# Sparse attention inside a hybrid layer: the products with the low parts of the keys contracted over 128 rows instead of 64

## The chip, the cores and the metric

One Trainium2 chip, one core of it. The metric is device time in microseconds (us) of one launch. The kernel before took 3008.09 us, the median of 3 runs (3004.27 to 3015.14). PE is TensorE (PEld its weight loads), DVE VectorE, ACT ScalarE, POOL GpSimd, SP SyncE; SPq is SP's DMA queue.

## What is computed

Two layers. Each layer norms 1104 token rows (16 meta tokens, 1024 prompt tokens, 64 sample tokens), projects them, and runs three branches: a gated linear recurrence, a convolution module, and an attention that keeps 256 keys a row by the scores of a small indexer. The parts of the reference that the change touches:

```
def index_scores(qi, wi, ki):
    s = jnp.einsum('bqhd,bsd->bqhs', qi.astype(F32), ki.astype(F32))
    return jnp.einsum('bqhs,bqh->bqs', jax.nn.relu(s), wi.astype(F32) * IDX_SCALE)
...
def sparse_attend(q, kg, vg, valid):
    nb, nq = q.shape[:2]
    qg = q.reshape(nb, nq, C_KV_HEADS, C_HEADS // C_KV_HEADS, C_HEAD_DIM).astype(F32)
    logits = jnp.einsum('bqhgd,bqnhd->bqhgn', qg, kg.astype(F32)) * (C_HEAD_DIM ** -0.5)
    logits = jnp.where(valid[:, :, None, None, :], logits, MASK_NEG)
    p = jax.nn.softmax(logits, axis=-1)
    o = jnp.einsum('bqhgn,bqnhd->bqhgd', p, vg.astype(F32))
    return o.reshape(nb, nq, C_WIDTH).astype(q.dtype)
```

A head has 64 channels (C_HEAD_DIM and IDX_DIM), there are 2 kv heads with 4 query heads each, and 4 index heads.

## The kernel before

**Split products.** All products keep float32 accuracy by halves: a value is split into a high part (rounded to fp32r) and a low part (what is left). A projection does three products for a tile: high with high, high with low, low with high. For queries and keys of 64 channels there is a denser form. The stationary operand is a *stack* of 128 rows, the high part of the query in one half of the rows and the low part in the other. The moving operand `KD` (`KIH` in the indexer) holds the high part of the keys in both halves, so one product over 128 rows gives (high + low query) x high key. A second product adds high query x low key: it takes the 64 rows of the stack with the high query, and the 64 rows of `KL` (`KIL`) with that head's low keys. It is this second product that contracts over 64 rows.

**Where it stands.** (1) `indexer`, lines 725 to 863: `qk` (768 to 771) writes the scores of one of 4 heads, for a tile of 128 query rows and up to 1024 keys, 512 at a time: line 770 is the product over 128 rows, 771 the one over 64. The row tiles go from i = 7 down to 2, with 128(i+1) keys each. `KIL` has the low keys in both halves already. Lines 861 and 862 do the same for the last 16 prompt rows. (2) `attention`, lines 945 to 1083: for i from 7 down to 0 and for the two kv heads k, `scores` (992 to 1016) does the 4 heads of the group, each in pieces of at most 512 keys (128 for i below 2); line 1004 is the product over 128 rows, 1005 the one over 64. `KL` is one tile: kv head 0 in rows 0 to 63, kv head 1 in 64 to 127. `queries(i)` (979 to 987) loads one tile of queries (`qr`, one buffer) and builds the stacks of both kv heads in one tile `Q`; it is called for i - 1 at the second kv head of i.

**Around it.** After a score piece DVE adds the mask and keeps the largest value (line 1011), from one of two PSUM banks (`sc`); ACT takes the exponential (204), DVE the reciprocal and the product with it (1014, 1015). `values` transposes the probabilities on PE (1023), ACT and DVE split them (1026, 1027) and PE multiplies them with the split values (1040, 1041). In the indexer ACT takes the relu (204, tile `rl`, two buffers) and DVE adds it up with its weight (803, 805); the taps of the convolution (1478, 1479) run on DVE in between.

**What sets the order.** PE's order is the program's, written by hand: tables of step counts (`FILL`, `SIDE`) say how many steps of the projections, three products each (line 391, later 326 to 328), stand behind each head's scores, each step of `values`, and so on. In `attention` DVE's order comes from a scheduler, as ACT's, POOL's and SP's do nearly everywhere; in the indexer DVE's is by hand too. Each queue runs strictly in its order.

Of the kernel before, what the change touches and what calls it, by code (L numbers as in the profile page):

```python
# [17 lines left out]
F32 = mybir.dt.float32  # L18
# [25 lines left out]
# steps of the projections that go at each place, and ns of the work of VectorE that does  # L44
# [18 lines left out]
def _layout():  # L63
# [11 lines left out]
    # channel-major, (half, chunk, kv head, 8) on the partitions  # L75
# [79 lines left out]
def trunk(tc, a, o, depth=DEPTH):  # L155
# [4 lines left out]
    def f(x):  # L160
        return x.bitcast(F32)
# [10 lines left out]
    # two banks, as one tile or as two  # L172
# [14 lines left out]
    def dmt():  # L187
        # where nothing else is under way: the slots of both tags
        return mmt() if next(turn) % 5 < 2 else tpt()
# [19 lines left out]
    # DRAM scratch  # L209
# [26 lines left out]
    # per-layer vectors, channel on the partition  # L236
# [5 lines left out]
    # lower bound of the gates of each layer  # L242
# [21 lines left out]
    def weights(l, blk, eng=None, pool=None):  # L264
        # 8 tiles of 128 x 128: the rows of one column chunk, or 4 row tiles of two column chunks
# [29 lines left out]
    class Early:  # L295
        # the products of the first two branches: they take the place of the rows, once no projection needs those
# [44 lines left out]
    def stream(l, pv, chunks, groups, slot, early, lead, more):  # L341
        # projections that wait in DRAM, one step (three products) at a time, after a first call for the weights alone;
        # the first `lead` chunks go by groups of tokens, as they are normalised, and so do the last two
# [19 lines left out]
        for i, g in parts:  # L363
# [16 lines left out]
            if i == 0:  # L380
                # the low parts of the rows come two of them behind
# [8 lines left out]
            for j, (w, x) in enumerate(ops):  # L390
                T.matmul(ps, w, x, start=(j == 0), stop=(j == 23))  # L391
                if j == 23:
                    # the gates of the first two branches as they are used, the others are activated later
                    fn = AF.Sigmoid if nm == "gate" and c < 16 else AF.Identity
                    act_(bufs[i][:, sl], ps, fn, bias=pv[:, bcol + c:bcol + c + 1])
                    if nm in ("cz",):
                        # stored as its silu
                        if g == 0:
                            sg = spt()
                        act_(sg[:, sl], ps, AF.Sigmoid, bias=pv[:, bcol + c:bcol + c + 1])  # L400
                        G.tensor_tensor(bufs[i][:, sl], bufs[i][:, sl], sg[:, sl], op=OP.mult)
# [8 lines left out]
    class Side:  # L410
        # work of VectorE that fits in anywhere, about `ns` of it at a time
# [42 lines left out]
    def inverse(parts, nn, tmp):  # L454
        # of the root of the mean square; roots and reciprocals are taken with the tokens on the partitions
# [19 lines left out]
    def norm_group(H, pv, g, r, tmp, pool="1357", lag=0):  # L475
        # a step for each row of tiles; the low parts `lag` of them behind
# [27 lines left out]
    def squares(g, out, lag=0):  # L504
        # the squares of a group of tokens, but for the last ones added up, `lag` of them behind
# [18 lines left out]
    def start(fill):  # L524
        # the first norm and the first projections, a group of tokens at a time
# [8 lines left out]
        for g in range(3):  # L534
            ahead = squares(g + 1, parts, 2) if g < 2 else iter(())
            for k, _ in enumerate(norm_group(H0, pvs[0][0], g, r, tmp0, "1346", 2)):
                next(ahead, None)
                # the rest of the products of the group before
# [15 lines left out]
    def constants():  # L554
        consts.update(cload(("rc", "rs", "cm80", "selw", "cols", "hsel", "bd", "p16"), "cb", S))
        # masks in fewer bytes: small numbers, or a far lower one
# [8 lines left out]
        # row of 8 cache slots held by partition p for sequence b: page_table[b, p // 16] * 16 + p % 16  # L565
# [7 lines left out]
    def layer(l, hst, late):  # L573
# [7 lines left out]
        # the last layer returns no outputs for the meta tokens  # L581
# [111 lines left out]
    def rope_q():  # L693
        # the rotated channels of all heads side by side, (half, chunk, kv head, 8) on the partitions
# [30 lines left out]
    def indexer(l, CTr, SC, SC8, fill, taps):  # L725
        with tc.tile_pool(name="ixc", bufs=1) as xc, tc.tile_pool(name="ixt", bufs=2) as xt:
# [3 lines left out]
            # high and low parts side by side  # L730
# [37 lines left out]
            def qk(dst, q, h, rows, c0, c1):  # L768
                j, e = divmod(h, 2)
                T.matmul(dst, q[:, j, e, 0:rows], KIH[:, c0:c1], start=True, stop=False)  # L770
                T.matmul(dst, q[64 * e:64 * e + 64, j, e, 0:rows], KIL[64 * e:64 * e + 64, c0:c1], start=False, stop=True)
# [37 lines left out]
            # last prompt rows and the sample rows  # L809
# [6 lines left out]
            # q stack of the tail rows: [hi; lo] for every head  # L816
# [43 lines left out]
            for (c0, c1), dst in zip(CH, (ps[0:64, 0:512], ps[0:64, 512:1024], px[0:64, 0:80])):  # L860
                T.matmul(dst, lq, KIH[:, c0:c1], start=True, stop=False)
                T.matmul(dst, lq[0:64], KIL[0:64, c0:c1], start=False, stop=True)
# [32 lines left out]
    def topk(SC, SC8, t1):  # L895
        # the 256th largest score of every row, bit by bit from the top of its float pattern
# [3 lines left out]
        def steps(j0, j1):  # L900
# [5 lines left out]
            for bit in range(31, -1, -1):  # L906
# [6 lines left out]
                # the bit stays, or goes back (the top one: to all ones); then the next one to try  # L913
# [7 lines left out]
    def topk_masks(SC, SC8, MB, MB8, F, t1):  # L921
        # 0 where a key is kept, MASK elsewhere; of equal scores the first ones are kept
# [22 lines left out]
    def attention(l, lo, MB, MB8, fill):  # L945
        with ExitStack() as st:
# [13 lines left out]
            KL = ac.tile([128, 1024], F32R, name="KL", tag="KL")  # L960
            for hf in range(2):
# [4 lines left out]
                for k in range(2):  # L966
# [3 lines left out]
                    V.tensor_tensor(KL[e, sl], ps[e], f(KD[k][e, sl]), op=OP.subtract)  # L970
            # high and low parts side by side: the rows of a head's own half of the products hold the high ones
# [7 lines left out]
            def queries(i):  # L979
                qr = at.tile([128, 4, 128], F32, name="qr", tag="qr", bufs=1)  # L980
                Y.dma_start(qr, fD["q"][:, :, 128 * i:128 * i + 128].rearrange("c p n -> p c n"))
                Q = at.tile([128, 2, 4, 128], F32R, name="Q", tag="Q")
                lo, hi = qr[0:64], qr[64:128]
                act_(Q[0:64, 0], lo, AF.Copy, scale=0.125)
                act_(Q[64:128, 1], hi, AF.Copy, scale=0.125)
                V.scalar_tensor_tensor(Q[64:128, 0], lo, 0.125, f(Q[0:64, 0]), op0=OP.mult, op1=OP.subtract)
# [772 lines left out]
```

## Time and profile before

| | |
|---|---|
| runs (us) | 3015.14, 3008.09, 3004.27; median 3008.09 |
| profiled execution, span | 3013.0 us, granted TensorE clock 0.980 on average |
| PE busy | 2881.1 us (96%), 17094 products |
| PEld busy | 2641.4 us (88%) |
| DVE busy | 2113.0 us (70%) |
| ACT, POOL busy | 1183.1 us (39%), 1250.3 us (41%) |
| line 1005 (attention, 64 rows) | 208 products, 88.8 us, mean 427 ns |

A busy PE is counted to the modelled end of each product, and products overlap, so its busy share says little of how closely they follow each other; the *starts* of two neighbours in the timeline do. The time of the profiled execution around its span is not listed apart; the highest of the three runs lies 2.1 us above the span, the median 4.9 us below it.

### The profile page before, as it was taken

The page shows a single profiled execution, that of the slowest core. Times are in us where ns is not written, and L with a number is a line of the kernel's source. Part 1 is how long each engine was busy: PE and PEld are TensorE (multiplying, and loading weights), DVE is VectorE, ACT ScalarE, POOL GpSimd, SP SyncE. Part 2 cuts the span into 40 slices and gives each one's busy share as a digit, 9 for nine tenths or more (in the row PEclk, how much of TensorE's full clock was granted, in tenths as well). Part 3 has the DMA queues.
Part 4 walks back from the last instruction along what each step waited for, and adds up shares of the span by engine and source line. Part 5 has one row for each costly group of instructions (what it writes and reads, how often), then busy time and mean ns, then how long its engine had stood idle before and what let it go on. Part 6 is the DMA issues. An engine that isn't in the chain of part 4 may idle for free. (4 is left out here: it accounts for less than half of the span.)

```text
span 3013.0 us, 44973 instructions
## 1 busy us (share of the span) xinstructions
PE 2881.1 (96%) x17094; PEld 2641.4 (88%) x17094; DVE 2113.0 (70%) x3824; ACT 1183.1 (39%) x2357; POOL 1250.3 (41%) x978
## 2 busy tenths in 40 slices
PE   8989999999999999989999999998999999999898
PEld 7988879999998888879999887898998988888798
DVE  5789768888978567444466895789898776664443
ACT  4323443333333456444441334422332244564432
POOL 3533334443434115746563332534452331157453
PEclk9999999999999999999999999999999999999999
DMA  4422333333244124655452312422331441246554
GB/s 150 150 82 83 102 107 128 113 122 115 82 154 149 59 81 138 209 170 185 156 165 79 110 66 100 157 74 99 122 132 64 155 142 58 76 146 209 170 159 152
DMA packets 192567, 374.13 MB, mean 124 GB/s; under 512 B 30656, under 2 KB 129696, under 8 KB 192288
## 3 DMA queue, kind: packets, MB, share of 16 engines
q1 hardware_dynamic: 166016, 272.21, 28.8%
q10 hardware_dynamic: 20448, 78.09, 6.4%
q0 software_dynamic: 5888, 20.97, 2.2%
q8 instruction: 134, 2.20, 0.3%
q14 instruction: 81, 0.66, 0.1%
HBM read 251.07 MB, written 122.40 MB: 124 GB/s over the span
## 5 line engine op out<-in xcount | busy, mean ns | idle before, releaser
L391 PE MATMUL mm<-xh,wh 128*128 128x384 f32 (+2 forms) x2656 | 891.8, 338 | 21.1 <-ACT sp L204 18.6
L391 PE MATMUL mm<-xl,wh 128*128 128x384 f32 (+2 forms) x2656 | 885.5, 336 | 0.0
L270 POOL TENSOR_TENSOR wl<-wr,wh 128x512 fp32r<-128x512 f32 x332 | 478.8, 1461 | 769.0 <-ACT wh L269 465.2
L391 PEld LDWEIGHTS mm<-xh,wh 128*128 128x128 f32 x2656 | 506.1, 191 | 38.9 <-ACT sp L204 22.9
L391 PE MATMUL mm<-xh,wl 128*128 128x384 f32 (+2 forms) x2656 | 533.8, 337 | 0.0
L391 PEld LDWEIGHTS mm<-xl,wh 128*128 128x128 f32 x2656 | 505.8, 190 | 7.6 <-issue 2.3
L391 PEld LDWEIGHTS mm<-xh,wl 128*128 128x128 f32 x2656 | 459.9, 192 | 9.5 <-issue 5.5
L910 DVE TENSOR_SCALAR_CACHE_REDUCE jk<-SC,F 80x1104 bf16<-80x1104 f32 (+6 forms) x448 | 448.7, 1002 | 8.4
L204 ACT ACTIVATE sp<-mm,vec 128x384 f32<-128x384 f32 (+1 forms) x356 | 198.6, 566 | 526.2 <-PE mm L391 509.4
L1478 DVE SCALAR_TENSOR_TENSOR cy<-up,vec,cy 128x1040 f32<-128x1040 f32 x240 | 329.2, 1372 | 0.4
L269 ACT CAST wh<-wr 128x512 fp32r<-128x512 f32 x352 | 203.9, 618 | 174.4 <-PE mm L391 90.4
L204 ACT ACTIVATE P<-P,nm 128x896 f32<-128x896 f32 (+7 forms) x128 | 99.6, 778 | 85.7 <-DVE nm L1011 84.5
L1027 DVE TENSOR_TENSOR pl<-tp,ph 128x512 fp32r<-128x512 f32 x144 | 98.2, 688 | 49.2 <-ACT ph L1026 48.7
L1479 DVE SCALAR_TENSOR_TENSOR cy<-us,vec,cy 128x64 f32<-128x64 f32 x240 | 123.3, 514 | 0.0
L1011 DVE CUSTOM_DVE_ANT_0 P<-sc,MB 128x512 f32<-128x512 f32 (+1 forms) x96 | 64.1, 668 | 80.5 <-PE sc L1005 80.3
L1026 ACT CAST ph<-tp 128x512 fp32r<-128x512 f32 x144 | 83.6, 584 | 89.0 <-PE tp L1023 85.6
L1329 PE MATMUL lg<-hQ,hK 128*128 128x64 f32 x512 | 68.5, 292 | 24.1 <-DVE hQ L1358 24.1
L1023 PE MATMUL tp<-ident,P 128*128 128x128 f32 x576 | 91.1, 280 | 0.5 <-DVE P L1015 0.5
L1329 PEld LDWEIGHTS lg<-hQ,hK 128*128 128x128 f32 x512 | 68.0, 210 | 26.3 <-issue 19.8
L1015 DVE TENSOR_SCALAR P<-P,nm 128x896 f32<-128x896 f32 (+7 forms) x128 | 85.8, 670 | 4.4
L1005 PE MATMUL sc<-KL,Q 64*128 64x512 f32 (+2 forms) x208 | 88.8, 427 | 0.0
L287 PE MATMUL tp<-xh,wh 128*128 128x384 f32 (+2 forms) x240 | 79.9, 335 | 0.4 <-DVE z L1664 0.4
(455 smaller groups left out, 5964.0 us busy)
## 6 DMA issues: line engine op xcount, KB each, us to landing
wr<-in_wp SPq DMA_DIRECT2D x180, 512.0 KB, 3.8
eg<-gateD SPq DMA_DIRECT2D x80, 184.0 KB, 3.0
gateD<-sp ACTq DMA_DIRECT2D x24, 552.0 KB, 2.7
gateD<-sp ACTq DMA_DIRECT2D x24, 544.0 KB, 2.7
cr<-in_wc SPq DMA_DIRECT2D x16, 290.0 KB, 3.2
gt<-gateD SPq DMA_DIRECT2D x24, 192.0 KB, 3.2
za<-zaD SPq DMA_DIRECT2D x24, 192.0 KB, 3.8
ggD<-sp ACTq DMA_DIRECT2D x8, 552.0 KB
```

What stands on the lines that cost most here:

```text
L204: S.activation(out, in_, fn, **kw)
L269: S.copy(wh[:, k:k + 4], wr[:, k:k + 4])
L270: (eng or G).tensor_tensor(wl[:, k:k + 4], wr[:, k:k + 4], f(wh[:, k:k + 4]), op=OP.subtract)
L391: T.matmul(ps, w, x, start=(j == 0), stop=(j == 23))
L910: V.tensor_scalar(jk[0:rows, 0:n], s, F.bitcast(F32)[0:rows, j:j + 1], None, op0=OP.is_ge, op1=OP.add, accum_out=cnt[0:rows, j:j + 1])
L1005: T.matmul(ps, Q[64 * k:64 * k + 64, k, c, :], KL[64 * k:64 * k + 64, c0:c1], start=False, stop=True)
L1015: V.tensor_scalar(p[:, 0:n], p[:, 0:n], nm[:, 3:4], None, op0=OP.mult)
L1023: T.transpose(ps[:, 128 * c:128 * c + 128], P[c][:, 128 * kt:128 * kt + 128], ident)
L1027: V.tensor_tensor(pl, ps, f(ph), op=OP.subtract)
L1329: T.matmul(ps[:, 64 * c:64 * c + 64], K[:, 128 * c:128 * c + 128], up(Q[:, 128 * c:128 * c + 128], m), start=True, stop=True)
L1478: V.scalar_tensor_tensor(yp, up[:, j:j + 1040], w, yp, op0=OP.mult, op1=OP.add)
L1479: V.scalar_tensor_tensor(ys, us[:, :, j:j + 8], w, ys, op0=OP.mult, op1=OP.add)
```

## The change

The second product of each pair runs over all 128 rows: the whole stack (high and low query) against the low keys in both halves. What it adds to the result is low query x low key. For the attention the low keys must stand in both halves for each kv head, so `KL` becomes two tiles `KL0`, `KL1` and each is written twice. The stack is built for one kv head at a time: `queries(i)` issues the load and gives back `halves`, which is called for k = 1 at the first kv head of i, and for k = 0 of i - 1, right after the load, at the second. `Q` keeps two buffers, each half as large. In the tail a scratch tile takes the place of `KL0` in place of `KL`. Comments went too, which moves line numbers from 965 on by 1, from 990 on by 4 and from 1064 on by 8.

```diff
             def qk(dst, q, h, rows, c0, c1):
                 j, e = divmod(h, 2)
                 T.matmul(dst, q[:, j, e, 0:rows], KIH[:, c0:c1], start=True, stop=False)
-                T.matmul(dst, q[64 * e:64 * e + 64, j, e, 0:rows], KIL[64 * e:64 * e + 64, c0:c1], start=False, stop=True)
+                T.matmul(dst, q[:, j, e, 0:rows], KIL[:, c0:c1], start=False, stop=True)
...
-                T.matmul(dst, lq[0:64], KIL[0:64, c0:c1], start=False, stop=True)
+                T.matmul(dst, lq, KIL[:, c0:c1], start=False, stop=True)
...
-            KL = ac.tile([128, 1024], F32R, name="KL", tag="KL")
+            KL = [ac.tile([128, 1024], F32R, name=f"KL{k}", tag=f"KL{k}") for k in range(2)]
...
                     V.tensor_copy(KD[k][64:128, sl], ps[e])
-                    V.tensor_tensor(KL[e, sl], ps[e], f(KD[k][e, sl]), op=OP.subtract)
+                    for d in (slice(0, 64), slice(64, 128)):
+                        V.tensor_tensor(KL[k][d, sl], ps[e], f(KD[k][d, sl]), op=OP.subtract)
...
-                Q = at.tile([128, 2, 4, 128], F32R, name="Q", tag="Q")
-                lo, hi = qr[0:64], qr[64:128]
-                act_(Q[0:64, 0], lo, AF.Copy, scale=0.125)
-                act_(Q[64:128, 1], hi, AF.Copy, scale=0.125)
-                V.scalar_tensor_tensor(Q[64:128, 0], lo, 0.125, f(Q[0:64, 0]), op0=OP.mult, op1=OP.subtract)
-                V.scalar_tensor_tensor(Q[0:64, 1], hi, 0.125, f(Q[64:128, 1]), op0=OP.mult, op1=OP.subtract)
-                return Q
+
+                def halves(k):
+
+                    Q = at.tile([128, 4, 128], F32R, name="Q", tag="Q")
+                    own, other = (slice(64 * e, 64 * e + 64) for e in (k, 1 - k))
+                    act_(Q[own], qr[own], AF.Copy, scale=0.125)
+                    V.scalar_tensor_tensor(Q[other], qr[own], 0.125, f(Q[own]), op0=OP.mult, op1=OP.subtract)
+                    return Q
+
+                return halves
...
-                    T.matmul(ps, Q[:, k, c, :], KD[k][:, c0:c1], start=True, stop=False)
-                    T.matmul(ps, Q[64 * k:64 * k + 64, k, c, :], KL[64 * k:64 * k + 64, c0:c1], start=False, stop=True)
+                    T.matmul(ps, Q[:, c, :], KD[k][:, c0:c1], start=True, stop=False)
+                    T.matmul(ps, Q[:, c, :], KL[k][:, c0:c1], start=False, stop=True)
...
-            Q = queries(7)
+            split = queries(7)
+            Q = split(0)
             fill("aq")
             for i in range(7, -1, -1):
                 oc = at.tile([128, 4, 128], F32, name="oc", tag="oc", bufs=1)
                 for k in range(2):
-                    if k:
-                        Qn = queries(i - 1) if i else None
+                    if k == 0:
+                        Qn = split(1)
+                    elif i:
+                        split = queries(i - 1)
+                        Qn = split(0)
...
-                Q = Qn
+                    Q = Qn
...
-            p = ac.tile([128, 1024], F32, name="p8", tag=("KL", "VS1")[gi % 2])
+            p = ac.tile([128, 1024], F32, name="p8", tag=("KL0", "VS1")[gi % 2])
```

PE's and POOL's instructions are as many as before, and PE's stand in the same order. The scheduler sets DVE, ACT and SP anew in the attention.

DVE, at the start of the attention of the first layer, from the first part of `KD` to the first mask of a score (`ISA`, line 1011, 1015 in the change). Before:

```order
L969 CAST KD_8532<-tp 64x512
L970 TENSOR_TENSOR KL<-tp,KD_8532 64x512
L969 CAST KD_8532<-tp 64x512
L970 TENSOR_TENSOR KL<-tp,KD_8532 64x512
L969 CAST KD_8533<-tp 64x512
L986 SCALAR_TENSOR_TENSOR Q<-qr,Q 64x512
L970 TENSOR_TENSOR KL<-tp,KD_8533 64x512
L969 CAST KD_8533<-tp 64x512
L987 SCALAR_TENSOR_TENSOR Q<-qr,Q 64x512
L970 TENSOR_TENSOR KL<-tp,KD_8533 64x512
L986 SCALAR_TENSOR_TENSOR Q<-qr,Q 64x512
L1011 ISA P,nm<-sc,MB 128x512
```

And in the change:

```order
L969 CAST KD_8532<-tp 64x512
L971 TENSOR_TENSOR KL_8534<-tp,KD_8532 64x512 x2
L969 CAST KD_8532<-tp 64x512
L971 TENSOR_TENSOR KL_8534<-tp,KD_8532 64x512
L969 CAST KD_8533<-tp 64x512
L971 TENSOR_TENSOR KL_8535<-tp,KD_8533 64x512 x2
L971 TENSOR_TENSOR KL_8534<-tp,KD_8532 64x512
L989 SCALAR_TENSOR_TENSOR Q<-qr,Q 64x512 x2
L969 CAST KD_8533<-tp 64x512
L971 TENSOR_TENSOR KL_8535<-tp,KD_8533 64x512 x2
L1015 ISA P,nm<-sc,MB 128x512
```

Four more subtractions into `KL` stand ahead of the first mask, and one piece of the stack less.

ACT, a little later in the same place, up to the second exponential (`P,nm<-P,nm`; `sp` are results of projections, `wh` high parts of weights). Before:

```order
L204 ACTIVATE Q<-qr 64x512
L269 CAST wh<-wr 128x512 x2
L204 ACTIVATE Q<-qr 64x512
L204 ACTIVATE sp<-mm,vec 128x336 x2
L204 ACT_TABLE_LOAD
L204 ACTIVATE P,nm<-P,nm 128x1024
L404 DMA czD<-sp 128x1104
L204 ACTIVATE P,nm<-P,nm 128x1024
```

And in the change:

```order
L204 ACTIVATE sp<-mm,vec 128x384 x2
L269 CAST wh<-wr 128x512 x2
L204 ACTIVATE sp<-mm,vec 128x336
L204 ACT_TABLE_LOAD
L204 ACTIVATE P,nm<-P,nm 128x1024
L204 ACT_TABLE_LOAD
L204 ACTIVATE sp<-mm,vec 128x336
L204 ACT_TABLE_LOAD
L204 ACTIVATE P,nm<-P,nm 128x1024
```

The stacks of the next row tile are gone from here; the first exponential comes between two `sp`, and two more loads of ACT's function table with it.

SP's queue, from the first output gate (`czt`) on. Before:

```order
L981 DMA qr<-qD 128x4x128
L1054 DMA czt<-czD 128x4x128
L267 DMA wr<-in_wp 128x1024
L981 DMA qr<-qD 128x4x128
L267 DMA wr<-in_wp 128x1024 x2
L1049 DMA ocD<-oc 128x4x128
L1054 DMA czt<-czD 128x4x128
L267 DMA wr<-in_wp 128x1024
L981 DMA qr<-qD 128x4x128
```

And in the change:

```order
L1058 DMA czt<-czD 128x4x128
L267 DMA wr<-in_wp 128x1024
L982 DMA qr<-qD 128x4x128
L267 DMA wr<-in_wp 128x1024 x2
L1053 DMA ocD<-oc 128x4x128
L1058 DMA czt<-czD 128x4x128
L982 DMA qr<-qD 128x4x128
L267 DMA wr<-in_wp 128x1024
```

The first `qr` of the rows before (the queries of tile 5) now stands behind that `czt` and a weight load, the second (tile 4) behind the store of an output (`ocD`) and the next `czt`; the third (tile 3) has left the piece.

## Rows read from the trace of the kernel before

**Rows 1.** The page's first part: span, and busy time of each engine.

```profile
span 3013.0 us, 44973 instructions
PE 2881.1 (96%) x17094; PEld 2641.4 (88%) x17094; DVE 2113.0 (70%) x3824; ACT 1183.1 (39%) x2357; POOL 1250.3 (41%) x978
```

**Rows 2.** Busy time by window: the first layer's indexer and attention.

```profile
core 0: us, PE busy (x) PEld busy (x) DVE busy (x) ACT busy (x) POOL busy (x), PEclk, DMA share, GB/s
230.00:336.00 106.00, 106.00 (x534) 88.41 (x534) 97.71 (x122) 40.71 (x72) 34.65 (x21) 1.00 0.24 81
956.00:1249.00 293.00, 290.46 (x1533) 242.24 (x1533) 180.31 (x437) 157.84 (x318) 94.81 (x78) 0.99 0.31 98
```

**Rows 3.** Waits, 956 to 1249 us: total us, times, longest us.

```profile
DVE P L1011 <- PE sc L1005: 52.6, 62, 3.2
...
PE sc L1004 <- DVE nm L1011: 0.5, 1, 0.5
```

**Rows 4.** One line's view: L1004 in 956 to 1249 us, L770 in the whole.

```profile
L1004 PE MATMUL sc<-KD,Q x104: 218/387/505, 956.0 to 1248.4; 128*128 128x512 f32 x48, 128*128 128x128 f32 x32, 128*128 128x384 f32 x16, 128*128 128x256 f32 x8
...
L770 PE MATMUL lg<-KIH,qs x80: 326/396/505, 230.0 to 1806.9; 128*128 128x512 f32 x48, 128*128 128x384 f32 x16, 128*128 128x256 f32 x8, 128*128 128x128 f32 x8
```

**Rows 5.** Timeline of PE, attention, i = 7: start, duration, line, tiles, rows*columns, shape.

```profile
986.06 0.39 PE L1004 MATMUL sc<-KD,Q 128*128 128x512 f32 x1
986.38 0.49 PE L1005 MATMUL sc<-KL,Q 64*128 64x512 f32 x1
986.80 0.49 PE L1004 MATMUL sc<-KD,Q 128*128 128x512 f32 x1
987.22 0.50 PE L1005 MATMUL sc<-KL,Q 64*128 64x512 f32 x1
987.65 0.66 PE L1023 MATMUL tp<-ident,P 128*128 128x128 f32 x4
988.06 0.48 PE L1040 MATMUL ac<-ph,VS 128*128 128x512 f32 x1
988.38 0.39 PE L1041 MATMUL ac<-pl,VS 128*128 128x512 f32 x1
988.61 0.34 PE L391 MATMUL mm<-xh,wh 128*128 128x384 f32 x1
```

**Rows 6.** Timeline of PEld, the same stretch.

```profile
986.38 0.18 PEld L1005 LDWEIGHTS sc<-KL,Q 64*128 64x128 f32 x1 [0.30 <-issue]
986.79 0.19 PEld L1004 LDWEIGHTS sc<-KD,Q 128*128 128x128 f32 x1 [0.24 <-issue]
...
988.15 0.19 PEld L1041 LDWEIGHTS ac<-pl,VS 128*128 128x128 f32 x1
```

**Rows 7.** Timeline of PE, the next such transposes, with no pair ahead of them.

```profile
989.67 0.60 PE L1023 MATMUL tp<-ident,P 128*128 128x128 f32 x4
...
990.56 0.34 PE L391 MATMUL mm<-xh,wh 128*128 128x384 f32 x1
990.74 0.34 PE L391 MATMUL mm<-xl,wh 128*128 128x384 f32 x1
```

**Rows 8.** Timeline of PE, i = 2: one pair of 384 columns, two projections.

```profile
1170.08 0.34 PE L1004 MATMUL sc<-KD,Q 128*128 128x384 f32 x1
...
1170.99 0.33 PE L327 MATMUL mm<-xl,wh 128*128 128x368 f32 x1
1171.15 0.33 PE L328 MATMUL mm<-xl,wl 128*128 128x368 f32 x1
```

**Rows 9.** Timeline of PE, i = 1: two pairs of 128 columns, one projection.

```profile
1197.22 0.22 PE L1004 MATMUL sc<-KD,Q 128*128 128x128 f32 x1
...
1198.41 0.33 PE L327 MATMUL mm<-xl,wh 128*128 128x368 f32 x1
```

**Rows 10.** Timeline of DVE, i = 6: the masks of one head's two pieces.

```profile
1001.76 0.69 DVE L1011 CUSTOM_DVE_ANT_0 P<-sc,MB 128x512 f32<-128x512 f32 x1 [0.73 <-PE sc L1005]
...
1002.60 0.62 DVE L1011 CUSTOM_DVE_ANT_0 P<-sc,MB,nm 128x384 f32<-128x384 f32 x1
```

**Rows 11.** Waits, 230 to 336 us.

```profile
DVE qs L764 <- ACT qs L763: 7.7, 4, 4.8
```

**Rows 12.** One line's view: L970, the low keys, on DVE.

```profile
L970 DVE TENSOR_TENSOR KL<-tp,KD x8: 682/689/695, 946.4 to 2448.0; 64x512 fp32r<-64x512 f32 x8
```

**Rows 13.** Timeline of ACT, first head of the attention.

```profile
959.81 1.28 ACT L204 ACT_TABLE_LOAD   x1
```

**Rows 14.** DMA issues: count, KB each, median us to landing.

```profile
qr<-qD SPq DMA_DIRECT2D x16, 256.0 KB, 3.0
```

**Rows 15.** Waits of SP's queue, 956 to 1249 us.

```profile
SPq L1049 <- POOL oc L1055: 32.7, 7, 21.1
```

## The prediction

> **What bounds the kernel now.** Read the page's first part before anything else: PE is counted busy for 96% of the span and DVE for 70% [rows 1]. That share is over all stages, so the next view is the busy time by window in the two stages that the change touches. There PE is busy for 106.00 of 106 us in the indexer and 290.46 of 293 in the attention of a layer, at a granted clock of 1.00 and 0.99 (the 2.4 GHz level); DVE is at 97.71 and 180.31 [rows 2]. Then the waits: in the attention DVE waits 52.6 us for line 1005, while PE waits for DVE's masks 0.5 us [rows 3]. So PE sets the pace in both stages, closely followed by DVE in the indexer and not in the attention.
>
> Next, how often the product with the low keys runs. Line 1004 and its partner 1005 come 104 times a layer, 48 times with 512 columns, 16 with 384, 8 with 256, 32 with 128; lines 770 and 771 come 80 times in both layers, 48, 16, 8 and 8 [rows 4].
>
> Last, what one pair costs, from the starts in PE's timeline. Two pairs of 512 columns at 986.06 and 986.80 hold PE until 987.65: starts 0.32, 0.42, 0.42 and 0.43 us apart. Yet lines 1040 and 1041, also 512 columns and also two products with the same stationary operand, show 0.23 from the second to its follower (988.38 to 988.61) [rows 5]. The weight loads tell why. Line 1041's load starts at 988.15, while line 1040, started at 988.06, is under way; those of 1005 and of the 1004 behind it start with their own product, after idle times of 0.30 and 0.24 us that the profile ascribes to nothing but issue [rows 6]. A load of the other row count waits until the product ahead is through, on the way into 64 rows and on the way back. That is the time the change can take.
>
> **What it removes.** I take the excess over the same rows without a switch. With four products at 0.23 the stretch from 986.06 to 987.65 (1.59 us) would take 0.92; the transposes and the value products behind it take 0.96 (987.65 to 988.61), and 0.89 where no pair stands ahead (989.67 to 990.56) [rows 5, 7]. So two pairs cost 0.67 + 0.07 = 0.74 too much, 0.37 a pair. For 384 columns: from the pair at 1170.08 through two projection products to 1171.15 is 1.07 us; at 0.17 for each of the four (a projection product of 384 columns follows its like by 0.18 [rows 7], one of 368 by 0.16 [rows 8]) it would be 0.68, an excess of 0.39 [rows 8]. For 128 columns: two pairs and one projection product take 1197.22 to 1198.41, 1.19 us; a product of 128 columns without a switch I put at 0.11, from four transposes in (0.89 - 0.46) / 4 [rows 7], so 4 x 0.11 + 0.16 = 0.60, an excess of 0.59, 0.29 a pair [rows 9]. For 256 columns I take 0.38, between its neighbours.
>
> Attention, a layer: 72 pairs of 256 columns or more x 0.38 + 32 x 0.29 = 27.4 + 9.3 = 36.7 us; two layers 73. Indexer, both layers: 80 x 0.39 (each head is followed by projections, so the price of rows 8) = 31 us. The six pairs of lines 861 and 862 I price likewise, 2 us. Gross 106 us.
>
> On the loads' overlap the Trainium skill says the opposite: "TensorE: Matmul & The Clock Gate", Part 3, has it that a weight load overlaps a running product only when their row groups differ. By that rule the wide product, which shares all rows with its partner, would expose its load as the narrow one does, and the gross sum would be 0 instead of 106. The trace disagrees: 1041's early load is of the same 128 rows [rows 6], and I take the trace.
>
> **What it adds.** The new second product has as many columns; its price of 0.23 is in the sum already. Losses, each against that sum:
>
> - *Masks of neighbouring heads.* The first two heads of a group stand nearly back to back on PE. With 0.46 a pair of pieces PE comes back to the two PSUM banks sooner than DVE has emptied them: a piece takes DVE 0.84 [rows 10]. Two heads of two pieces need 2 x 0.92 + 0.5 of projection work on PE, against 1.4 us until the first bank and 2.3 until the second is free; a wait of 0.3 to 0.5 us for i = 7, 6, 5, both kv heads: 2.4 us a layer, 5 in all. Below: nothing, where fill steps cover it; above: 0.84 for each of 16 groups and two layers, 27.
> - *Indexer and DVE.* DVE is busy 97.71 of 106 us there and idle 8.3, of which 7.7 is waiting for ACT's share of the query stacks, itself behind PE [rows 2, 11]. Without 15.6 us of PE's time (half of 31) DVE becomes the later one. It can trail PE by some two heads, about 8 us (two buffers `rl`), and catch up in the stage behind, so I let PE lose 3.5 us a layer, 7 in all. Bounds: 0, and all but the idle 8.3, 2 x (15.6 - 8.3) = 15; if also the 7.7 stay, 30.
> - *Twice the writes of the low keys.* Four more subtractions of 0.69 a layer, 2.8 us [rows 12], on DVE ahead of the first mask. One piece of the stack left that place, and the first pair needs only `KL0`, so I put this at 0; bounds 0 and 6 for two layers.
> - *ACT's order.* Two more function table loads a layer at 1.28 [rows 13], between the first two exponentials. PE waits for the second `sp` behind them only if it is late by more than a head's 4 us; I take 0.5 a layer, bounds 0 and 5 in all.
> - *The stacks one kv head at a time.* The same 16 copies and 16 subtractions a layer, none more. `qr` has one buffer, so the load of i - 1 now waits until the second half of i is read; it is still issued a whole group before its use, and takes 3.0 us [rows 14]. Cost 0; the case that it isn't is a rival.
> - Shorter cover for the two finished branches that are loaded into the rows' place at i = 3: 1 us a layer by choice, bounds 0 and 8.
>
> Net: 106 - 5 - 7 - 0 - 1 - 0 - 2 = **91 us**. Nothing behind these stages gives it back: the tail of the attention and the top-k steps start from results of PE, and shift with them. Against the profiled execution, whose span is 3013.0 and which I put at 3015 (the highest run), that is 2924; against the median of the runs, 3008, it is **2917 us**.
>
> **The rivals.**
> - *DVE takes the indexer.* For: DVE at 92% there [rows 2]. Against: the stage behind lets it catch up. If nothing is left of the 31, and the mask waits are twice mine, the gain is 55 to 60: 2950.
> - *No loss anywhere*, the gross sum: 2902. Against: DVE's 0.84 a piece [rows 10] is longer than PE's new 0.46.
> - *The load isn't hidden after all*, because of the shared stationary rows: the pairs stay at 0.37 too much, and only the small additions count: 3008, at most 3014. Against: lines 1040 and 1041 [rows 6]. The rule of the Trainium skill's "TensorE: Matmul & The Clock Gate", Part 3, would give this case.
> - *Slower, by the queries' load.* It is now issued later, behind stores of outputs on SP's queue, which waits for POOL up to 21.1 us at a time there [rows 15]. If the load lands that late, ACT stands before its copy, with exponentials behind it, and PE stands for the probabilities. There are 14 such loads; beyond 91 / 14 = 6.5 us each the change loses. At 10 us each: 3008 - 91 + 140 = 3057. Against: a group of heads lasts 10 to 25 us and the load is issued at its beginning.
>
> **How the numbers follow.** Forecast 0.62, DVE takes the indexer 0.20, no loss 0.10, load not hidden 0.04, slower 0.04. A measurement of this kernel tells some 0.3%, 9 us, from no change. Faster by more than that are the first three, 0.92; within it the fourth, 0.04; slower the last, 0.04. The range runs from just under the gross sum, 2898, to the rival with DVE and a little of ACT's bounds, 2952.
>
> **What would show it.** Right: in PE's timeline of the changed kernel four products of two 512-column pairs start 0.23 apart; the second product's loads show no idle time put down to issue; the attention's stretch goes from 293 us to about 260, the indexer's from 106 to 94; PE has small new waits for DVE's masks, under 1 us each. Wrong: starts still 0.42 apart (the load isn't hidden); PE idle for `rl` or the query stacks for more than 5 us in an indexer (DVE); PE idle in the attention with ACT behind `qr` (the slower rival).

## The result and the profile after

The changed kernel takes 2936.41 us, the median of four runs (2933.32 to 2938.49), beside 3006.18 us for the kernel before in as many. The ratio is 0.9764, with a 95% interval from 0.9747 to 0.9782: some 70 us less. The forecast was 2917 us, 91 less; the result lies in its range, 19 us above the forecast. The profiled execution is the slowest of the four, and so is the one of before; their spans are 76.4 us apart.

The first part of the page, changed kernel (answers to [rows 1]; PE has the same number of products):

```profile
span 2936.6 us, 44992 instructions
...
PE 2783.8 (95%) x17094; PEld 2628.5 (90%) x17094; DVE 2116.7 (72%) x3832; ACT 1189.9 (41%) x2361; POOL 1248.6 (43%) x978
```

Busy time by window, the indexer and the attention, each in both layers (answers to [rows 2]):

```profile
core 0: us, PE busy (x) PEld busy (x) DVE busy (x) ACT busy (x) POOL busy (x), PEclk, DMA share, GB/s
226.50:322.00 95.50, 90.53 (x520) 86.40 (x521) 92.06 (x121) 39.19 (x71) 32.20 (x20) 1.00 0.25 86
1668.00:1764.00 96.00, 91.08 (x524) 86.94 (x523) 91.92 (x122) 39.09 (x71) 31.25 (x20) 1.00 0.25 87
945.00:1212.00 267.00, 260.51 (x1538) 240.25 (x1537) 180.44 (x440) 162.17 (x321) 94.98 (x79) 0.99 0.34 108
2405.00:2671.00 266.00, 258.83 (x1540) 238.95 (x1539) 181.62 (x440) 161.66 (x321) 94.56 (x79) 0.99 0.34 108
```

The granted clock is what it was. Both stages are shorter, and in both PE now has gaps: 5.0 us in an indexer in which DVE is busy for 92 of 95.5, and 6.5 us in an attention, where it had 2.5.

The timeline of PE in the attention at i = 7, the place that answers to [rows 5], and of its loads (to [rows 6]). Columns: start, duration, line, tiles, rows*columns, shape, count.

```profile
971.40 0.39 PE L1008 MATMUL sc<-KD,Q 128*128 128x512 f32 x1
971.63 0.39 PE L1009 MATMUL sc<-KL,Q 128*128 128x512 f32 x1
971.86 0.40 PE L1008 MATMUL sc<-KD,Q 128*128 128x512 f32 x1
972.09 0.39 PE L1009 MATMUL sc<-KL,Q 128*128 128x512 f32 x1
972.33 0.60 PE L1027 MATMUL tp<-ident,P 128*128 128x128 f32 x4
972.68 0.48 PE L1044 MATMUL ac<-ph,VS 128*128 128x512 f32 x1
```

```profile
971.40 0.19 PEld L1009 LDWEIGHTS sc<-KL,Q 128*128 128x128 f32 x1
971.63 0.19 PEld L1008 LDWEIGHTS sc<-KD,Q 128*128 128x128 f32 x1
971.86 0.19 PEld L1009 LDWEIGHTS sc<-KL,Q 128*128 128x128 f32 x1
```

The four starts are 0.23 us apart, where [rows 5] have 0.32 to 0.43; the load of 1009 starts at 971.40, with the product *ahead* of its own. This is the first step of the prediction, as it was put.

PE's new waits. In the attention of the first layer, 945 to 1212 us (total us, times, longest us; answers to [rows 3]):

```profile
DVE P L1015 <- PE sc L1009: 34.0, 40, 2.0
...
PEld sc L1008 <- DVE nm L1015: 6.5, 16, 0.8
PEld ac L1045 <- DVE pl L1031: 6.4, 8, 2.5
```

In the indexer, 226 to 322 us (answers to [rows 11]):

```profile
ACT rl L204 <- DVE SC L805: 31.6, 11, 3.5
...
PEld lg L770 <- ACT rl L204: 5.6, 5, 1.9
PE lg L770 <- ACT rl L204: 4.1, 4, 1.6
```

In the indexer DVE's sum (805) is late, so ACT's relu has no buffer `rl` to write, so PE has no bank for the next head's scores. In the attention the waits for the masks were foreseen; those of line 1045 for `pl` were not.

**Stages.** From the first product to the last line of a stage, by the starts in the two profiled executions: each indexer (first start of 770 to line 861) went from 168.5 to 160.1 us, 16.8 in both layers; the attention (first to last 1008) from 292.4 to 266.1 and from 292.8 to 264.4, 54.7 in both; the six pairs of lines 861 and 862 from 3.62 to 2.02. That is 73.1 of the spans' 76.4; the rest lies in stages that the change doesn't touch. By the windows (the indexer's ends with its row tiles) the stretches are 95.5 and 267 us long, where the prediction had 94 and about 260.

### The profile page after: what moved, and what is told of

The parts are those of the page before. It is cut to its first block, busy times and chain, and to the rows that moved or that the text cites. A ratio compares the mean times of both kernels' runs of the same rounds, so it can differ in the third digit from the quotient of the medians.

```text
span 2936.6 us, 44992 instructions
## 1 busy us (share of the span) xinstructions
PE 2783.8 (95%) x17094; PEld 2628.5 (90%) x17094; DVE 2116.7 (72%) x3832; ACT 1189.9 (41%) x2361; POOL 1248.6 (43%) x978
## 5 line engine op out<-in xcount | busy, mean ns | idle before, releaser
L270 POOL TENSOR_TENSOR wl<-wr,wh 128x512 fp32r<-128x512 f32 x332 | 472.1, 1439 | 697.8 <-ACT wh L269 436.6
L1337 PEld LDWEIGHTS lg<-hQ,hK 128*128 128x128 f32 x512 | 66.3, 206 | 25.1 <-issue 21.8
L204 ACT ACTIVATE rl<-lg 128x1024 f32<-128x1024 f32 (+6 forms) x54 | 42.6, 789 | 105.1 <-DVE SC L805 67.6
```

The costliest lines, as they stand in the source:

```text
L204: S.activation(out, in_, fn, **kw)
L270: (eng or G).tensor_tensor(wl[:, k:k + 4], wr[:, k:k + 4], f(wh[:, k:k + 4]), op=OP.subtract)
L1337: T.matmul(ps[:, 64 * c:64 * c + 64], K[:, 128 * c:128 * c + 128], up(Q[:, 128 * c:128 * c + 128], m), start=True, stop=True)
```

## The experiments

All ratios are to the kernel before, run on the same chip beside it; several chips were used, so kernels are compared by their ratios.

**One part at a time.** First the indexer alone:

```diff
-                T.matmul(dst, q[64 * e:64 * e + 64, j, e, 0:rows], KIL[64 * e:64 * e + 64, c0:c1], start=False, stop=True)
+                T.matmul(dst, q[:, j, e, 0:rows], KIL[:, c0:c1], start=False, stop=True)
...
-                T.matmul(dst, lq[0:64], KIL[0:64, c0:c1], start=False, stop=True)
+                T.matmul(dst, lq, KIL[:, c0:c1], start=False, stop=True)
```

> The kernel before with the indexer's second products (lines 771 and 862) on 128 rows, the attention as before. Theory A (a switch of the row count costs 0.37 to 0.39 us a pair, and the changed kernel's indexer gave back part of it to waits for DVE): the indexer from its first product to line 861 goes from 168.5 us to about 160 in each layer, as in the trace of the changed kernel, the tail's six pairs give 2 more, so 3006 - 17 - 2 = 2987, and PE waits for `rl` about 5 us a layer. Theory B (DVE is the whole limit of the indexer, and the changed kernel gained there by something else): 3004 to 3006. No loss at all would give 3006 - 33 = 2973.

Measured: 2987.05 us, ratio 0.9937 (0.9915 to 0.9959), 19 us less. The stage takes 160.2 and 160.0 us, as in the changed kernel. Theory A.

Then the attention alone: the changed kernel with those two lines as they were.

> The changed kernel with the indexer's second products back on 64 rows: only the attention is changed. Theory A: the attention's stretches go from 292.5 us to about 265, as in the changed kernel, 26 and 28 us: 3006 - 54 = 2952. Together with the run that changes the indexer alone the gains must then add up to the whole 70. Theory B (the stages share a limit, such as DVE's top-k steps behind both): the two gains add up to clearly more or less than 70, by 10 us or over.

Measured: 2955.87 us, ratio 0.9824 (0.9802 to 0.9846), 53 us less; the attention takes 266.9 and 265.2 us. 19 and 53 make 72, against 71 by the ratio of the whole change: the two parts add up.

**The layout without the rows.** The changed kernel, the indexer's lines as before, and in the attention:

```diff
-                    T.matmul(ps, Q[:, c, :], KL[k][:, c0:c1], start=False, stop=True)
+                    T.matmul(ps, Q[64 * k:64 * k + 64, c, :], KL[k][64 * k:64 * k + 64, c0:c1], start=False, stop=True)
```

> The changed kernel with every second product back on 64 rows, in the indexer and in the attention, but with the queries split one kv head at a time, `KL0` and `KL1`, and the low keys written twice. Theory A (the row count alone pays, the layout costs nothing): 3006, within 6 us. Theory B (the layout itself takes or gives time, by DVE's extra subtractions, ACT's table loads or the later load of the queries): 3012 to 3025, or 2990 if the smaller stacks help.

Measured: 3008.24 us in ten runs, ratio 0.9994 (0.9982 to 1.0007). The split of the queries, the low keys written twice, ACT's table loads and the later load of `qr` together cost nothing that can be measured, with the narrow products in place. The 70 us come from the row count alone.

**Is it the change of the row count, or the narrow product?** The kernel before, all second products on 64 rows, but the products of a head with two pieces in another order (other heads, and the masks behind the products, as before):

```diff
+                if len(parts) == 2 and i >= 2:
+                    pss = [pair[0].tile([128, 512], F32, name="sc", tag="sc")[:, 0:c1 - c0] for c0, c1 in parts]
+                    for ps, (c0, c1) in zip(pss, parts):
+                        T.matmul(ps, Q[:, k, c, :], KD[k][:, c0:c1], start=True, stop=False)
+                    for ps, (c0, c1) in zip(pss, parts):
+                        T.matmul(ps, Q[64 * k:64 * k + 64, k, c, :], KL[64 * k:64 * k + 64, c0:c1], start=False, stop=True)
...
```

> The kernel before, all second products still on 64 rows; only for heads of two pieces (i = 7 to 4, 32 heads a layer) the two wide products of a head come first and its two narrow ones behind them, so a head changes the row count twice in place of four times. Theory A (the change of the row count costs, whatever the narrow product does): 64 pairs of switches less at 0.37 = 24 us, less up to 5 of waits for the second bank: 2982 to 2987. Theory C (the narrow product itself is slow, or the wide one behind it, at any order): 3006; a wait for the second bank ahead of the first narrow product could make it up to 10 slower.

Measured: 2999.29 us in ten runs, ratio 0.9976 (0.9966 to 0.9987), 7 us less: faster as theory A has it and C has not, but by less than half of the 24. The timelines of PE and of its loads in this kernel, one head of i = 7 (lines 1005 and 1007 are the wide and the narrow product):

```profile
988.51 0.62 PE L1005 MATMUL sc<-KD,Q 128*128 128x512 f32 x2
989.06 0.73 PE L1007 MATMUL sc<-KL,Q 64*128 64x512 f32 x2
989.72 0.55 PE L1034 MATMUL tp<-ident,P 128*128 128x128 f32 x3
```

```profile
988.34 0.36 PEld L1005 LDWEIGHTS sc<-KD,Q 128*128 128x128 f32 x2
989.06 0.29 PEld L1007 LDWEIGHTS sc<-KL,Q 64*128 64x128 f32 x2 [0.36 <-issue]
989.72 0.42 PEld L1034 LDWEIGHTS tp<-ident,P 128*128 128x128 f32 x4 [0.36 <-PE sc L1007]
```

From the first wide start to the transposes it is 1.21 us, against 1.59 in [rows 5]: 0.38 less for one pair of switches less, the price of the prediction. Idle time ahead of a load stands only where the row count changes, once on the way into 64 rows and once back. The two loads of 64 rows are through 0.29 us after 989.06, with the first narrow product (0.34 us to the start of the second) still under way: a load of 64 rows does go beside a running product of 64 rows. So it is neither the narrow product nor its load that is slow, but the change. Where the rest of the 24 went: added up over the starts, the score products of both attentions fell by 16.8 us. The second wide product now needs the second bank before the first narrow one may go, and waits for DVE's mask (5.8 us over the usual 0.23 in the 64 heads). The two attentions take 568.2 us here, 17.0 less than in the profile of before, which is the slowest of its four runs, and 12 to 14 less than in the two later profiles with the products of before (580.0 and 582.6). Why the runs show 7 is left open.

The Trainium skill's "TensorEngine Tiling (Array Packing)", section Key Properties, has it that a change of the tiling mode drains the engine; this trace agrees: the first narrow load comes only after 0.36 us of idle time, with its own product, and there and back cost 0.38 us. The sentence of the Trainium skill's "TensorE: Matmul & The Clock Gate", Part 3, that a load overlaps a running product only where their row groups differ, is contradicted by the loads of 1009 above, which start beside a product of the same 128 rows.

**Any other row count, or 64?**

```diff
-                    T.matmul(ps, Q[:, c, :], KL[k][:, c0:c1], start=False, stop=True)
+                    T.matmul(ps, Q[0:96, c, :], KL[k][0:96, c0:c1], start=False, stop=True)
```

> The changed kernel with the attention's second product on rows 0 to 95 only: it leaves out the share of the last 32 rows. Theory A (what costs is the change from 128 rows to 64 and back, not any unequal count): the starts of 512-column products stay 0.23 apart and the time is that of the changed kernel, 2936, within 5. Theory B (any other row count makes the load wait): 0.42 apart, and the attention's 51 us are given back: 2987 to 2995.

Measured: 2939.68 us, ratio 0.9762 (0.9747 to 0.9778), the changed kernel's own. PE's timeline:

```profile
976.70 0.39 PE L1008 MATMUL sc<-KD,Q 128*128 128x512 f32 x1
976.92 0.40 PE L1009 MATMUL sc<-KL,Q 96*128 96x512 f32 x1
977.16 0.40 PE L1008 MATMUL sc<-KD,Q 128*128 128x512 f32 x1
977.40 0.40 PE L1009 MATMUL sc<-KL,Q 96*128 96x512 f32 x1
```

From 128 rows to 96 and back costs nothing that shows. Of the two counts that were run, only 64 costs.

**What the indexer lost.** The changed kernel without the convolution's steps between the indexer's heads:

```diff
-        "tk": 4200, "ti": (1400, 2800, 2800, 2800, 2800, 2800), "ts": 3000,
+        "tk": 4200, "ti": 0, "ts": 3000,
```

> The changed kernel with none of the convolution's steps on DVE between the heads of the indexer (the entry ti of the table SIDE is 0): they are done behind the indexer instead, so only the stage is read and not the whole time, which may rise by tens of us. Starts in the traces say that the pairs and the products behind them became 29.3 us shorter in both indexers (56.1 + 11.7 before, 31.3 + 7.2 after), 14.7 a layer, while the stage gave 8.4. Theory A (DVE, busy there for 92 of 95.5 us, keeps the rest): without the steps the stage from the first product to line 861 goes from 160.1 to 168.5 - 14.7 = 153.8, within 1 us, and PE no longer waits for `rl`. Theory B (ACT's own chain or the query stacks keep it): 158.5 to 160.

Measured: the stage takes 153.6 and 153.5 us, and PE has no gap left. By window:

```profile
232.00:320.00 88.00, 88.00 (x516) 85.70 (x517) 28.80 (x45) 39.88 (x71) 20.05 (x20) 1.00 0.26 87
```

So DVE kept 160.1 - 153.6 = 6.5 us a layer. The whole took 3063.18 us (one run): the steps, 61.6 us a layer by the table, came behind the indexer, and the stretch from line 861 to the attention grew from 558.4 to 626.3 us in the first layer. Then only a part of them was moved, to the gathers of the sampled keys:

```diff
-        "tk": 4200, "ti": (1400, 2800, 2800, 2800, 2800, 2800), "ts": 3000,
+        "tk": 4200, "ti": (1000, 2400, 2400, 2400, 2400, 2400), "ts": 4200,
```

> The changed kernel with 0.4 us less of the convolution's steps on DVE behind each of the indexer's 24 heads (about 9.6 us a layer), and as much more of them behind the gathers of the sampled keys, where the entry ts goes from 3.0 to 4.2 us. Theory A (DVE's overload of some 5 us a layer makes PE wait): the stage up to line 861 goes from 160.1 to 155 to 157, and the time from 2936 to 2927 to 2931, if the gathers hide the steps. Theory B (it only moves the wait to the gathers or to the query stacks): 2936, within 4.

Measured: 2930.91 us, ratio 0.9733 (0.9719 to 0.9746), 0.0031 or 9 us less than the changed kernel's; the stage takes 155.5 us, and the gathers hide what was moved (from line 861 to the attention 558.5 us, beside 558.4). And further:

```diff
-        "tk": 4200, "ti": (1400, 2800, 2800, 2800, 2800, 2800), "ts": 3000,
+        "tk": 4200, "ti": (700, 2100, 2100, 2100, 2100, 2100), "ts": 5100,
```

> The changed kernel with 0.7 us less of the convolution's steps behind each of the indexer's heads, and the entry ts from 3.0 to 5.1 us, to find where the shift of DVE's work stops paying. The run without any steps there ends the stage after 153.6 us, the one with 0.4 us less after 155.5. Theory A (the wait is DVE's all the way): 153.6 to 154.2 a layer, 2 to 4 us less than the run with 0.4 us less, 2927 to 2929. Theory B (the gathers can't hide 17 us more of DVE a layer): the stage is as short, but the time is 2931 or more.

Measured: **2919.94 us** (2916.09 to 2927.67), ratio 0.9714 (0.9699 to 0.9730). The stage takes 153.5 us, as without any steps. By the ratios this is 86 us less than before and 15 less than the changed kernel; the stages explain 13 of the 15 (2 x 6.6). Against the run with 0.4 us less it is 6 us by the ratios and 4 by the stages, and the intervals of the two overlap.

```profile
232.00:321.00 89.00, 89.00 (x524) 86.89 (x523) 80.43 (x102) 40.37 (x72) 29.46 (x20) 1.00 0.27 91
```

PE is busy all the time again, and DVE for 90% of it.

**What the attention lost.** The longest new wait is at i = 3, where the two finished branches are loaded and split while scores and values go on. PE, DVE and POOL in the changed kernel:

```profile
1129.42 0.50 PE L1044 MATMUL ac<-ph,VS 128*128 128x512 f32 x1 [0.34 <-ACT ph L1030]
1132.14 0.55 PE L1045 MATMUL ac<-pl,VS 128*128 128x512 f32 x1 [2.22 <-DVE pl L1031]
```

```profile
1129.29 2.19 DVE L308 TENSOR_TENSOR xl<-xl 128x736 fp32r<-128x736 f32 x1
1131.41 0.68 DVE L1031 TENSOR_TENSOR pl<-tp,ph 128x512 fp32r<-128x512 f32 x1
```

```profile
1128.96 1.74 POOL L308 TENSOR_TENSOR xl<-xl 128x736 fp32r<-128x736 f32 x1 [0.98 <-ACT xl L306]
```

DVE, in its order, does its half of a split (308) ahead of the `pl` for which PE waits. The first try took it off DVE:

```diff
-                for e, k in ((V, 0), (G, 2)):
+                for e, k in ((G, 0), (G, 2)):
```

> The changed kernel with the low parts of the two finished branches (line 308) all on POOL, none on DVE. In the trace of the changed kernel DVE spends up to 2.19 us on one of them while PE waits for `pl` behind it: 3.7 and 4.5 us of waits at i = 3 in the two layers, 2.0 and 0.8 before the change. Theory A (these are the waits that the shorter cover uncovered): they go, and the time falls from 2936 by 6 to 8, to about 2929. Theory B (POOL takes 5 us in place of 2.5 for one part, and the branches' products wait for it): 2936 to 2945, with waits of lines 326 and 327 for POOL.

Measured: 2941.30 us, ratio 0.9766 (0.9752 to 0.9780): no gain. The wait for `pl` became one for `ph` (waits of PE, 940 to 1212 us, and ACT's timeline):

```profile
PE ac L1044 <- ACT ph L1030: 3.6, 1, 3.6
PE mm L327 <- POOL xh L308: 0.6, 1, 0.6
```

```profile
1135.63 1.42 ACT L306 CAST xl<-xl 128x1472 fp32r<-128x1472 f32 x1 [3.13 <-DMA xl<-obD]
1136.96 1.06 ACT L1030 CAST ph<-tp 128x512 fp32r<-128x512 f32 x2
```

Theory B in its outcome. The wait of line 327 for POOL that it named is there too, but small; the larger one comes of ACT, which stands 3.13 us for the branch's load, with two copies `ph` behind it. The second try left the loads where they were and took the two parts some steps later:

```diff
             for X, src in ((XH, oaD), (XL, obD)):
-                hi, low = X[:, 0:4, sl], X[:, 4:8, sl]
-                Y.dma_start(f(low), src[:, :, sl].rearrange("c p n -> p c n"))
-                S.copy(hi, f(low))
+                Y.dma_start(f(X[:, 4:8, sl]), src[:, :, sl].rearrange("c p n -> p c n"))
+
+        def split(self, g):
...
             if nm == "early":
+                if i == n and g == 1:
+                    early.split(2)
...
+                if i == n - 2 and g and j == 11:
+                    early.split(g - 1)
```

> The changed kernel with only the loads of the two finished branches where they were; their high and low parts are taken some projection steps later, and on ACT the third group's two copies then stand behind the two `ph` copies that stood behind them. Theory A (ACT, in order, stands for a late load, and PE for `ph` and `pl` behind it): the wait of 2.5 us that each layer has at i = 3 goes, the waits at i = 3 fall from 4.0 and 5.0 to about 1.5 and 2.5, and the time falls by 4 to 6, from 2936 to 2931. Theory B (the wait moves to the branches' products, lines 334 to 336 of this kernel, since the copies come later): 2936, within 3.

Measured: 2935.95 us, ratio 0.9764 (0.9746 to 0.9782): no gain, theory B. The waits for `pl` at i = 3 fell to 1.2 and 1.6 us, as A has it, but by the starts PE now waits 3.4 and 3.2 us there for the branches' products (waits of PE, 940 to 1212 us; 330 is this kernel's 326, 1053 its 1045):

```profile
PE mm L330 <- ACT xh L310: 1.9, 1, 1.9
PE ac L1053 <- DVE pl L1039: 1.9, 4, 1.1
```

The kernel before has such waits too (waits of PE, 940 to 1249 us):

```profile
PE mm L327 <- DVE xh L308: 0.5, 1, 0.5
PE mm L327 <- POOL xh L308: 0.3, 1, 0.3
PE mm L326 <- ACT xh L306: 0.2, 1, 0.2
```

By the starts PE waits 4.4 us for the branches' products at i = 3 in both layers of the kernel before, and not at all in the changed kernel, where the waits for `ph` and `pl` stand in their place. All waits over 0.2 us at i = 3 together are 5.8 us before, 8.7 in the changed kernel and 9.6 here. So most of the waiting there is for the branches' data or behind the work on them; which part of their way is too slow isn't shown.

With the steps of the first move on top:

> The run with the later copies and the run with 0.4 us less of the convolution's steps behind each of the indexer's heads, put together. If the two waits are separate their gains add up: 5 of the one and 5 to 9 of the other, 2922 to 2926. If the time that the indexer gives back comes out later in the same place, not under 2930.

Measured: 2928.56 us, ratio 0.9734 (0.9715 to 0.9752): the gain of the moved steps alone, as the run before gave none to add. Last the masks, on top of this one:

```diff
-        "c1": (13, 22, 52), "aq": 16, "av": (2, 2, 2, 2, 2, 1, 3, 2), "a0": 6, "as": (3, 1, 1, 1, 2, 1, 0, 1),
+        "c1": (13, 22, 52), "aq": 16, "av": (2, 2, 2, 2, 2, 1, 2, 2), "a0": 6, "as": (3, 1, 1, 1, 2, 1, 2, 1),
```

> The run that puts both together, with two more projection steps behind each of the eight heads of i = 6 (the entry as[6] from 0 to 2) and one less beside each of the value steps there (av[6] from 3 to 2), so that about as many steps are done in all. Theory A (two heads of i = 6 stand so close on PE that DVE's masks are late, 1.6 us a layer with 0.6 at one place): these waits go and nothing takes their place, 3 us less than the run that puts both together. Theory B (the value products need the steps more than the masks): the waits for `ph` and `pl` at i = 6 grow by as much or more, the same time or up to 10 us more.

Measured: 2945.23 us, ratio 0.9791 (0.9771 to 0.9811), 17 us more than the run that it stands on. The mask waits of i = 6 went, and the attention stayed as long (267.1 and 263.8 us beside 266.4 and 264.6), with waits at i = 1 and i = 3 in their place. The loss lies behind the attentions: in the profiled executions the stretches from an attention's last score product to the next indexer and to the end took 6.4 and 5.7 us more than in the run that it stands on. The sums of steps weren't quite equal, 9 products fewer in each attention and 9 more behind it; why that costs so much was not followed up.

## Why the prediction was right in kind and 21 us too high in gain

Measured sizes are from the two profiled executions: the starts of all pairs and of the product behind each, taken at the median of their shape (so without waits; where all of a shape wait, as the four second pieces of i = 6 with another head right behind them do, at the median of their like), and, for waits, the intervals more than 0.2 us longer than usual. What is taken as usual moves single waiting terms by some 1 us. The terms, both layers, us:

| term | predicted | measured |
|---|---|---|
| attention, pairs at the new price | 73 | 70.9 |
| indexer, pairs | 31 | 29.3 |
| six pairs of lines 861, 862 | 2 | 1.6 |
| masks of neighbouring heads | -5 | -3.4 |
| indexer, DVE | -7 | -12.5 |
| shorter cover at i = 3 (7.4 of new waits, 4.4 of old ones gone) | -2 | -3.0 |
| products waiting for `ph` and `pl` at the other i | not in the sum | -4.2 |
| waits under 0.2 us and the rest, by difference to the stages | not in the sum | -5.6 |
| ACT's order, double low keys, queries | -1 | 0 |
| sum | 91 | 73.1 |

- **The price of a pair** was right: 102 us measured for 106. It was less even than forecast: matched product by product, a pair of 256 columns gave 0.45 us in the attention and 0.49 in the indexer, where 0.38 and 0.39 were put, and in the attention a pair of 512 columns gave 0.28 with another pair right behind it and 0.41 with other work behind. Excess over like rows without a switch, read from starts, was the right measure. That the load is hidden, on the strength of lines 1040 and 1041 [rows 6], held, and the rival that it isn't fell.
- **Masks**: foreseen place, right kind, smaller than priced. Heads of i = 7, 6 and 5 wait, up to 0.6 us each, most of it at i = 6.
- **DVE in the indexer**: the mechanism was right and the size wrong. The step "It can trail PE by some two heads ... and catch up in the stage behind, so I let PE lose 3.5 us a layer" failed: starts without waits are 29.3 / 2 = 14.7 us a layer shorter, the stage 8.4, so 6.3 were lost, and the run without DVE's steps gave 6.5. Nothing was caught up in the stage behind: from the last 770 to line 861 it takes 66.3 us before, 65.8 after and 65.9 without the steps, and the whole loss lies among the row tiles. The upper estimate of 15 for both layers, from DVE's idle time [rows 2], was nearer. PE's gaps of 5.0 and 4.9 us in the two windows stand at the limit of 5 that the prediction set as the sign of its rival (DVE takes the indexer, 2950), which overshot as well; that rival's terms, 106 - 31 - 10 - 1 - 2, make a gain of 62 and not 55 to 60.
- **The cover at i = 3** was priced at 1 us a layer "by choice", and by luck that is near: 3.0 for 2, the difference of new waits and of old ones that are gone. That it was the only term of its kind is the second step that failed. The prediction asked whether PE comes to a *score* sooner than its bank is free, but not the same of a *value product*: waits for `ph` and `pl` grew by 4.2 us at the other i as well, and small waits and the rest took 5.6 more. That ACT and DVE need the same time as before for `ph` and `pl`, with less of PE's work between the transposes and the products that use them, fits these rows, but no run isolates it. Two tries to mend i = 3 moved the wait and did not shorten it; it isn't shown what would.
- **Layout**: 0 was right, by the run that changes nothing else. The slower rival (the queries' load) is gone with it.
- **Against the runs**: the two stages and the six pairs, and so the table, give 73.1, the runs 70. The profiled execution of before is the slowest of its four, and its attention (292.4 and 292.8 us) is above that of the two later profiles that have the same attention products (290.5 and 292.1 with the indexer changed, 291.6 and 288.4 with the layout alone).

## What to carry to other kernels

A product over 64 rows between products over 128 rows cost 0.24 to 0.49 us here for the way there and back, by place and columns; filling it up to 128 rows, or to 96, cost nothing and gave that back, and where it can't be filled up, put the narrow ones behind each other (7 us here). When PE is sped up in a stage where another engine is at 92% of it, count on that engine's idle time as all that you get (8.3 us idle, 8.4 gained), and move its work to a neighbouring stage in the same edit: here that was worth 15 us more. And when a stage is shortened, ask of every pair of neighbours in PE's order, not only of those that were edited, what time the engines between them had.

## What the runs showed of the hardware that was not expected

- A load of 64 rows goes beside a running product of 64 rows (both loads through 0.29 us after the first narrow start), and products of 96 rows follow those of 128 at 0.23 us. The cost hangs on the change between 64 rows and 128, not on unequal counts as such.
- The split of line 308 takes DVE 2.19 us at 1129.29 and 0.93 at 1114.13, for the same shape. At 1129.29 POOL had begun the other half 0.33 us earlier, for 1.74 us; at 1114.13 DVE began first, and POOL took 2.52:

```profile
1114.13 0.93 DVE L308 TENSOR_TENSOR xl<-xl 128x736 fp32r<-128x736 f32 x1 [1.11 <-ACT xl L306]
```

```profile
1114.17 2.52 POOL L308 TENSOR_TENSOR xl<-xl 128x736 fp32r<-128x736 f32 x1 [10.44 <-ACT xl L306]
```

  Whoever begins second is done about 0.8 us (DVE) or 1.6 us (POOL) after the other, as if it stood for the whole of the other's instruction. The Trainium skill's "SBUF — State Buffer", section SBUF: two separate sides, says this of a DVE operation with two inputs in SBUF beside one of GpSimd; these four rows agree.
